# Channel mix, second product: its 98 factor loads issued from ScalarE's queue instead of SyncE's

## The chip, the cores and the metric

One core of one Trainium2 chip runs the program. The metric is the device time of one execution in microseconds (us); the kernel before was run three times.

## What is computed

Two blocks follow each other on a sequence of 1024 tokens of width 1024. The first is a recurrent mixer. The second has two layers (an RWKV-7 time mix, then a differential attention), and each layer ends in the same channel mix, which is where the change is:

```
def _sqrelu_mlp(x, w1, w2):
    return jnp.square(jax.nn.relu(x @ w1)) @ w2
...
x = _layer_norm(ALPHA * x + _sqrelu_mlp(x, mlp_w1[l], mlp_w2[l]), ln_g[l, 1], ln_b[l, 1], LN_EPS)
```

w1 is 1024 x 4096 and w2 is 4096 x 1024. Everything is float32.

## The kernel before

Every float32 product is made of three matmuls: each factor is split into a high and a low part, by a cast on ScalarE (ACT, L112) and a subtraction on VectorE (DVE, L113), and high x high, high x low and low x high are summed in PSUM.

`tail` holds a layer's channel mix and is called once for each of the two layers. Of the 4096 hidden columns, 512 go through a plain product (`direct`). The other 3584 stand in NC = 7 chunks of 512, and both products of a chunk are made by a scheme with seven products of half-size blocks in place of eight, the function `pair`: p1, p5, p2, p6, p3, and late p7 and p4, each a run of matmuls at L1549 into a PSUM bank (psx, psy or psz). Some of these sums are needed twice, so ACT copies them out of PSUM (`snap`, L1556) before TensorE (PE) goes on adding to the same bank.

- **First product** (x @ w1). Its sinks (`up_sink`) apply relu and square, form the seven sums that the second product wants as right factors, split them, and store each one to DRAM as `hd[chunk, factor]` (`parts_to`, L1500, on SyncE's queue, SP). Two stores of 512 KB make one factor of 1 MB.
- **Second product** (hidden @ w2). For each chunk, `rights(c)` loads the seven right factors from `hd` into a ring of 10 and later 12 buffers of 1 MB (names `tm`, `mxl`, `hx` in the profile): seven loads a chunk, 49 a layer, 98 in all, at L1686. The left factors come from w2 (`down_raw`, L1619, SP's queue), are summed on POOL (`lefts`, L1522) and split on ACT and DVE into `wc`. Every chunk makes four pairs of seven products of six matmuls. A buffer of the ring can be loaded again when all four pairs of its chunk have read it. The two `hx` buffers lie where the first product kept sums that it stores, so they can be filled only when those stores have landed.

A scheduler sets the order of the instructions of each engine when the program is built, and each engine then runs its own list in order. A DMA's wait is on the issuing engine's list too: what stands behind it on that engine waits with it. Completions are counted on eight semaphores in turn (`DMAHW0` to `DMAHW7` below), shared by the queues; a DMA that takes one waits until the last DMA on it has landed.

Lines that the text speaks of: L1686 the loads, L1500 the stores to `hd`, L1619 the weights of the second product, L1549 its matmuls, L1556 the copies out of PSUM, L112 the casts, L1727 the first chunk's copies into the result, L1774 eight loads of the plain product's hidden columns (`hpd`), which the change does not touch.

Of the kernel before, what the change touches and what calls it, by code (L numbers as in the profile page):

```python
# [6 lines left out]
F32 = mybir.dt.float32  # L7
# [72 lines left out]
class Net:  # L80
# [1248 lines left out]
    def tail(self, fx, wa, srcd, pre, pd, w, resd, ln1, w1, w2, ln2, outd, feats, xd, hd, hpd):  # L1329
# [8 lines left out]
        nc = self.nc  # L1338
# [4 lines left out]
        with ExitStack() as ctx:  # L1343
# [335 lines left out]
            def rights(c):  # L1679

                out = [None] * 7

                def step(i):
                    r = ring[at["ring"] % len(ring)]
                    at["ring"] += 1
                    nc.sync.dma_start(out=r.bitcast(F32), in_=hd[c, i].rearrange("p k x t -> p (k x t)"))  # L1686
                    out[i] = r.rearrange("p (k x t) -> p k x t", k=2, x=2)

                return out, [lambda i=i: step(i) for i in range(7)]
# [81 lines left out]
            for f in range(4):  # L1771
                r = ring[at["ring"] % len(ring)]
# [649 lines left out]
```

## Time and profile before

| what | value |
|---|---|
| median of 3 runs | 3378.27 us |
| lowest and highest | 3369.55 and 3382.08 us |
| the profiled execution | 3369.63 us |
| its span, first to last instruction | 3367.6 us |
| PE busy | 95% of the span |
| ACT busy | 51% |
| DVE busy | 67% |

The profile is of one execution. In the rows below, PE is the matmul engine, ACT is ScalarE, DVE VectorE, POOL GpSimd, SP SyncE; an engine's name with a q is its sequencer, as in SPq for a DMA that SP issues. Times in a timeline are microseconds from the span's start. The second product of the first layer lies at about 1735 to 2010, that of the second layer at about 3005 to 3285.

### The profile page before, as it was taken

What the parts mean: (1) busy time and instruction counts of PE and PEld (TensorE: products, weight loads), DVE (VectorE), ACT (ScalarE), POOL (GpSimd) and SP (SyncE); (2) the same over time, 40 slices, a digit from 0 to 9 for tenths busy, and PEclk for the clock granted to TensorE, in tenths of its full rate; (3) what the DMA queues carried; (4) which work ended last, traced back from release to release, by engine and by line L of the source; (5) the groups of instructions that cost most, each with busy time, mean ns of one, the idle gap of its engine ahead of it and who ended that gap; (6) DMA issues with size and microseconds to landing.
All of it is one profiled execution on the core that took longest, in us unless ns stands there. A gap on an engine that the chain in (4) does not pass through costs nothing. (4 is left out here: it accounts for less than half of the span.)

```text
span 3367.6 us, 51242 instructions
## 1 busy us (share of the span) xinstructions
PE 3193.2 (95%) x19242; PEld 2697.0 (80%) x19242; DVE 2261.9 (67%) x4255; ACT 1705.3 (51%) x3212; POOL 586.6 (17%) x463
## 2 busy tenths in 40 slices
PE   7999999989998988999999999999999999999998
PEld 5787899778777887888777887888998788777886
DVE  6645567758894867777775768226667677775777
ACT  5844235656764444466663334226566566663332
POOL 1000000000012220032224650000000032224660
PEclk9999999989997888999999999999999999999999
DMA  3110313335369655246689654544447336679653
GB/s 105 44 44 26 112 61 129 104 100 170 113 175 210 155 145 195 89 148 225 231 295 349 237 217 152 181 133 110 123 121 223 115 126 238 235 271 364 246 219 113
DMA packets 432871, 559.82 MB, mean 166 GB/s; under 512 B 114272, under 2 KB 327680, under 8 KB 419056
## 3 DMA queue, kind: packets, MB, share of 16 engines
q1 hardware_dynamic: 431792, 555.73, 50.9%
q8 instruction: 152, 2.49, 0.3%
q14 instruction: 95, 0.78, 0.1%
q0 software_dynamic: 544, 0.33, 0.0%
q10 hardware_dynamic: 288, 0.49, 0.0%
HBM read 368.25 MB, written 188.22 MB: 165 GB/s over the span
## 5 line engine op out<-in xcount | busy, mean ns | idle before, releaser
L1549 PE MATMUL psx<-tm,wc 128*128 128x512 f32 x1392 | 345.8, 390 | 4.7 <-DMA tm<-hd 2.4
L1549 PEld LDWEIGHTS psx<-tm,wc 128*128 128x128 f32 x1392 | 261.1, 188 | 62.9 <-issue 3.2
L113 DVE TENSOR_TENSOR wl<-wr,wh 128x1024 fp32r<-128x1024 f32 (+1 forms) x168 | 181.1, 1084 | 164.2 <-ACT wh L112 158.2
L112 ACT CAST wh<-wr 128x1024 fp32r<-128x1024 f32 (+1 forms) x168 | 153.9, 927 | 265.5 <-PE pskq L154 62.5
L1549 PE MATMUL psx<-mxl,wc 128*128 128x512 f32 x656 | 197.9, 390 | 0.4 <-DVE acc L100 0.4
L113 DVE TENSOR_TENSOR wc<-wr,wc 128x512 fp32r<-128x512 f32 x168 | 137.8, 823 | 51.2 <-ACT wc L112 51.2
L1549 PE MATMUL psz<-tm,wc 128*128 128x512 f32 x672 | 166.2, 389 | 0.0
L112 ACT CAST wc<-wr 128x512 fp32r<-128x512 f32 x168 | 103.6, 619 | 120.3 <-PE psz L1549 58.5
L113 DVE TENSOR_TENSOR wc<-x,wc 128x512 fp32r<-128x512 f32 x112 | 112.6, 1009 | 64.8 <-ACT wc L112 64.2
L1481 POOL TENSOR_TENSOR xx<-xx 128x512 f32<-128x512 f32 x8 | 12.0, 1498 | 820.4 <-DVE rsy L109 660.7
L153 PE MATMUL psmm<-uh,wh 128*128 128x512 f32 x384 | 152.7, 398 | 2.2 <-ACT uh L112 1.7
L1549 PE MATMUL psx<-mxh,wc 128*128 128x512 f32 x448 | 149.8, 395 | 4.4 <-DVE xx L100 4.3
L155 PE MATMUL psmm<-uh,wl 128*128 128x512 f32 x384 | 150.6, 392 | 0.5 <-DVE wl L113 0.5
L154 PE MATMUL psmm<-ul,wh 128*128 128x512 f32 x384 | 150.6, 392 | 0.5 <-DVE ul L113 0.5
L1549 PEld LDWEIGHTS psz<-tm,wc 128*128 128x128 f32 x672 | 126.2, 188 | 26.5
L1549 PEld LDWEIGHTS psx<-mxl,wc 128*128 128x128 f32 x656 | 123.0, 188 | 26.7 <-DVE acc L100 1.5
L100 DVE TENSOR_TENSOR acc<-acc,psx 128x512 f32<-128x512 f32 x144 | 96.2, 679 | 69.7 <-PE psx L1549 69.6
L993 POOL MEMSET pt<- 128x8 f32 x16 | 2.1, 128 | 724.9 <-PE psg L624 589.5
L1522 POOL TENSOR_TENSOR x<-wr 128x512 f32<-128x512 f32 x56 | 75.4, 1357 | 287.2 <-DMA wr<-in_mlp_w_dram 285.3
L112 ACT CAST wc<-x 128x512 fp32r<-128x512 f32 x112 | 69.7, 624 | 105.6 <-POOL x L1522 95.3
L97 ACT ACTIVATE e<-pss,mx 128x256 f32<-128x256 f32 (+7 forms) x128 | 94.9, 745 | 46.9 <-DVE mx L2070 26.9
L1549 PEld LDWEIGHTS psx<-mxh,wc 128*128 128x128 f32 x448 | 84.1, 188 | 29.3 <-DVE xx L100 12.1
(613 smaller groups left out, 9702.5 us busy)
## 6 DMA issues: line engine op xcount, KB each, us to landing
wr<-in_mlp_w_dram SPq DMA_DIRECT2D x128, 512.0 KB, 5.5
hd<-xx SPq DMA_DIRECT2D x112, 512.0 KB, 6.5
tm<-hd SPq DMA_DIRECT2D x50, 1024.0 KB, 7.9
mxl<-hd SPq DMA_DIRECT2D x32, 1024.0 KB, 8.1
hd<-ln SPq DMA_DIRECT2D x56, 512.0 KB, 4.0
hx<-hd SPq DMA_DIRECT2D x16, 1024.0 KB, 6.9
hd<-junk SPq DMA_DIRECT2D x28, 512.0 KB, 5.5
wr<-in_w_in_dram SPq DMA_DIRECT2D x24, 512.0 KB, 3.7
```

The source lines that it names most:

```text
L97: self.nc.scalar.activation(out=out, in_=in_, func=func, **kw)
L100: self.nc.vector.tensor_tensor(out=out, in0=a, in1=b, op=op)
L112: self.nc.scalar.copy(out=hi, in_=src)
L113: self.nc.vector.tensor_tensor(out=lo, in0=src, in1=hi.bitcast(F32), op=ALU.subtract)
L153: nc.tensor.matmul(out=ps, lhsT=ah, rhs=bh, start=first and i == 0, stop=False)
L154: nc.tensor.matmul(out=ps, lhsT=ah, rhs=bl, start=False, stop=False)
L155: nc.tensor.matmul(out=ps, lhsT=al, rhs=bh, start=False, stop=last and i == n - 1)
L993: nc.gpsimd.memset(pt[:, :, 0:1], 1.0)
L1481: nc.gpsimd.tensor_tensor(out=b0, in0=b1, in1=b0, op=ALU.subtract)
L1522: nc.gpsimd.tensor_tensor(out=s[k], in0=a, in1=b, op=op)
L1549: nc.tensor.matmul(out=ps, lhsT=a, rhs=b, start=first and k == 0 and n == 0, stop=k == nk - 1 and n == 2, skip_group_check=True,)
```

## The change

The one instruction that issues a load of a right factor moves from SP's queue to ACT's. The stores of `hd`, the loads of the weights and the loads of `hpd` stay on SP's.

```
                 def step(i):
                     r = ring[at["ring"] % len(ring)]
                     at["ring"] += 1
-                    nc.sync.dma_start(out=r.bitcast(F32), in_=hd[c, i].rearrange("p k x t -> p (k x t)"))
+
+                    nc.scalar.dma_start(out=r.bitcast(F32), in_=hd[c, i].rearrange("p k x t -> p (k x t)"))
                     out[i] = r.rearrange("p (k x t) -> p k x t", k=2, x=2)
```

Lines behind the change stand one higher in the new kernel (L1686 is L1687 there). The scheduler places the loads anew. Three places of the built programs, all in the first layer; in brackets is what a row waits for.

The first is ACT's list where the first product ends (`xx`, `ln`, `keep` are sums to be stored, `x` are copies from PSUM, `wc` left factors). Before:

```order
L112 CAST wc<-x_13045 128x512 [waits PE_49,Pool_49]
L112 CAST xx_13051<-xx_13051 128x512 [waits Activation_49]
L1556 COPY x_13043<-psz 128x512 [waits PE_49]
L112 CAST wc<-wr 128x512
L112 CAST xx_13052<-keep 128x512 [waits DMAHW4_49,DVE_49]
L112 CAST xx_13051<-xx_13051 128x512 [waits DMAHW5_49,DVE_49]
```

And with the change:

```order
L112 CAST wc<-x_13045 128x512 [waits PE_49,Pool_49]
L112 CAST xx_13051<-xx_13051 128x512 [waits Activation_49]
L1687 DMA tm_13059<-hd 128x2048 [waits PE_49]
L1556 COPY x_13043<-psz 128x512 [waits PE_49]
L112 CAST xx_13052<-keep 128x512 [waits DMAHW4_49,DVE_49]
L112 CAST wc<-wr 128x512
L1687 DMA tm_13059<-hd 128x2048
L112 CAST xx_13051<-xx_13051 128x512 [waits DMAHW5_49,DVE_49]
```

The layer's first two loads now stand behind this cast of `xx` and beside this copy of psz.

The second is SP's list at the same place, before:

```order
L1500 DMA hd<-xx_13052 128x1024 [waits DMAHW0_49,DVE_49]
L1500 DMA hd<-ln_13047 128x1024 [waits DMAHW1_49,DVE_49]
L1686 DMA tm_13059<-hd 128x2048 [waits DMAHW2_49,PE_49]
L1686 DMA tm_13059<-hd 128x2048 [waits DMAHW3_49,PE_49]
L1500 DMA hd<-ln_13048 128x1024 [waits DMAHW4_49,DVE_49,Activation_49]
L1500 DMA hd<-xx_13051 128x1024 [waits DMAHW5_49,DVE_49]
```

And with the change:

```order
L1500 DMA hd<-xx_13052 128x1024 [waits DMAHW0_49,DVE_49]
L1500 DMA hd<-ln_13047 128x1024 [waits DMAHW1_49,DVE_49]
L1500 DMA hd<-ln_13048 128x1024 [waits DMAHW4_49,DVE_49,Activation_49]
L1500 DMA hd<-xx_13051 128x1024 [waits DMAHW5_49,DVE_49]
L1500 DMA hd<-xx_13052 128x1024 [waits DMAHW6_49,DVE_49]
```

Nothing takes the two loads' place on SP: the next entry is the store of `ln` that waits for DVE and ACT.

The third is ACT's list where the second chunk's factors are fetched (`acc` is the result). Before:

```order
L1727 COPY acc<-psx 128x512 [waits PE_49]
L1556 COPY x_13044<-psx 128x512 [waits DVE_49,PE_49]
L112 CAST wc<-wr 128x512 [waits DMAHW1_49]
L112 CAST wc<-wr 128x512
L1727 COPY acc<-psx 128x512 [waits PE_49]
```

And with the change:

```order
L1728 COPY acc<-psx 128x512 [waits PE_49]
L1556 COPY x_13044<-psx 128x512 [waits DVE_49,PE_49]
L1687 DMA tm_13060<-hd 128x2048 [waits DMAHW2_49]
L1687 DMA hx_16477<-hd 128x2048 [waits DMAHW5_49,DMAHW3_49]
L1687 DMA mxl<-hd 128x2048 [waits DMAHW4_49,PE_49]
L1687 DMA mxl<-hd 128x2048 [waits DMAHW5_49,PE_49]
L112 CAST wc<-wr 128x512 x2
L1728 COPY acc<-psx 128x512 [waits PE_49]
```

Four loads, with their waits for earlier DMAs, now stand ahead of two casts of left factors.

## Rows read from the trace of the kernel before

**Rows 1.** The page's head and its list of DMA issues (count, size, median to landing)

```profile
span 3367.6 us, 51242 instructions
...
wr<-in_mlp_w_dram SPq DMA_DIRECT2D x128, 512.0 KB, 5.5
...
tm<-hd SPq DMA_DIRECT2D x50, 1024.0 KB, 7.9
```

**Rows 2.** What waited for the loads at L1686: engine, group, us, times

```profile
  PE psx L1549: 13.4, 4
```

**Rows 3.** Stretches, first layer: length, busy us by engine, PE clock, DMA share, GB/s

```profile
1735.00:1740.00 5.00, 4.97 (x23) 3.78 (x22) 2.08 (x3) 2.41 (x4) 4.84 (x4) 1.00 1.01 333
...
1750.00:1760.00 10.00, 7.60 (x31) 5.47 (x30) 7.76 (x13) 7.52 (x14) 0.00 (x0) 1.00 1.02 406
...
1800.00:1810.00 10.00, 4.44 (x14) 3.27 (x13) 1.20 (x3) 1.36 (x3) 3.05 (x3) 0.83 1.02 422
1810.00:1820.00 10.00, 10.00 (x44) 7.84 (x43) 5.21 (x8) 2.35 (x4) 3.43 (x3) 1.00 0.68 258
...
1840.00:1960.00 120.00, 120.00 (x527) 98.63 (x526) 87.87 (x108) 40.63 (x70) 72.03 (x50) 1.00 0.67 243
```

**Rows 4.** PE's timeline, both layers: start, us, line, out<-in, count, idle before

```profile
1744.77 4.24 PE L1549 MATMUL psx<-tm,wc 128*128 128x512 f32 x18
...
1798.04 2.43 PE L1549 MATMUL psz<-mxl,wc 128*128 128x512 f32 x10
1806.03 4.38 PE L1549 MATMUL psx<-hx,wc 128*128 128x512 f32 x12 [5.56 <-DMA hx<-hd]
...
3076.24 5.46 PE L1549 MATMUL psx<-hx,wc 128*128 128x512 f32 x12 [5.45 <-DMA hx<-hd]
```

**Rows 5.** SP's timeline, first layer

```profile
1734.24 1.47 SPq L1686 DMA_DIRECT2D tm<-hd  x2
1742.60 0.32 SPq L1500 DMA_DIRECT2D hd<-ln  x1
...
1790.39 0.32 SPq L1686 DMA_DIRECT2D hx<-hd  x1
...
1796.03 0.38 SPq L1619 DMA_DIRECT2D wr<-in_mlp_w_dram  x1
...
1801.28 2.09 SPq L1619 DMA_DIRECT2D wr<-in_mlp_w_dram  x1
```

**Rows 6.** Issue to landing of the loads issued at 1734.2 to 1734.9

```profile
DMA to landing us min/median/max: 7.3/8.2/9.1
```

**Rows 7.** The same for the second layer's first two, issued at 3004.5 to 3005.0

```profile
DMA to landing us min/median/max: 7.6/8.5/9.5
```

**Rows 8.** The same for the 23 loads issued between 1840 and 1980

```profile
DMA to landing us min/median/max: 4.7/6.9/9.0
```

**Rows 9.** ACT's timeline: the cast and copy around the first load's new place; a DMA issue of ACT's own

```profile
1740.74 0.62 ACT L112 CAST xx<-xx 128x512 fp32r<-128x512 f32 x1
1741.26 0.58 ACT L1556 COPY x<-psz 128x512 f32<-128x512 f32 x1
...
1.19 0.46 ACTq L179 DMA_DIRECT2D cst<-in_c_cst_dram  x1
```

**Rows 10.** Waits over the span: of SP at L1686, of POOL for the weights (us, times, longest)

```profile
SPq L1686 <- PE psx L1549: 142.3, 38, 10.1
...
POOL x L1522 <- DMA wr<-in_mlp_w_dram: 285.3, 25, 22.0
```

**Rows 11.** ACT's timeline: a copy and two casts behind later loads' new places

```profile
1769.31 0.58 ACT L1556 COPY x<-psz 128x512 f32<-128x512 f32 x1
...
1788.12 1.14 ACT L112 CAST wc<-wr 128x512 fp32r<-128x512 f32 x2
```

**Rows 12.** SP's timeline: the loads that stand ahead of them in the new list

```profile
1775.68 0.51 SPq L1686 DMA_DIRECT2D tm<-hd  x1
...
1792.60 1.24 SPq L1686 DMA_DIRECT2D mxl<-hd  x2
```

More of the change, by code (lines that the diff above doesn't have):

```diff
@@ L1685, in step @@
                     at["ring"] += 1
-                    nc.sync.dma_start(out=r.bitcast(F32), in_=hd[c, i].rearrange("p k x t -> p (k x t)"))
+                    nc.scalar.dma_start(out=r.bitcast(F32), in_=hd[c, i].rearrange("p k x t -> p (k x t)"))
                     out[i] = r.rearrange("p (k x t) -> p k x t", k=2, x=2)
```

## Prediction

> **What bounds the kernel now.** I read PE's share first, then what PE waits for in the second product, then the DMA engines there, and last the queue's own list. The span is 3367.6 us [rows 1], and the profiled execution took 3369.63 us. In the steady part of the second product, 1840 to 1960, PE is busy 120.00 of 120 us, while ACT works 40.63 of 120 [rows 3]: PE sets the pace, and nothing that arrives sooner helps. All that PE ever waited for these loads is 13.4 us in 4 waits [rows 2]. Two of them matter, one in each layer: PE stands 5.56 us before 1806.03 and 5.45 us before 3076.24 until the factor `hx` has landed [rows 4]. The reader is to see why `hx` is late. It was issued at 1790.39 [rows 5] and landed just before 1806.03, over 15 us later, where the 23 loads of the steady part take 4.7 to 9.0 us [rows 8]. The DMA engines are the reason: their share is 1.01 at 1735 to 1740, 1.02 at 1750 to 1760 and still 1.02 at 1800 to 1810, and falls to 0.68 only after 1810 [rows 3]. So from about 1735 to 1806 `hx` lies behind a backlog, and its landing is set by how much work the DMA engines have done by then.
>
> **The change part by part.** Against the profiled execution; the second layer repeats the pattern, so each term counts twice.
>
> *The first two loads start later.* SP issued them at 1734.24 and within 1.47 us [rows 5]; it then had nothing to issue until the store at 1742.60, which waits for ACT and DVE. On ACT they stand behind the cast that starts at 1740.74 and takes 0.62 us [rows 9], so the first goes out at 1741.36 at the earliest, 7.1 us later. In between the DMA engines, at 333 GB/s and a share of 1.01 [rows 3], lose these two loads as work, and SP has nothing else to give them. What is lost is two services. The two land 7.3 and 9.1 us after issues 0.6 us apart [rows 6], that is 1741.5 and 1744.0, 2.45 us apart; in the second layer 7.6 and 9.5 us after issues 0.5 apart give 2.4 [rows 7]. Two times 2.45 is 4.9 us. Since the engines have no gap until after `hx`, I take the whole 4.9 us as the shift of its landing: the wait goes from 5.56 to 10.5 us, and from 5.45 to 10.4. Bounds per layer: 0 if the hole is filled some other way, 7.1 us if the whole delay is carried on; I take 4.9, since the backlog is made of services, not of delays. **Twice 4.9 is +9.8 us.**
>
> *PE's start on the chunk.* The first load's reader is the run of psx matmuls that starts at 1744.77 [rows 4]; two matmuls in, it needs the buffer. Landing at 1741.36 plus 4.7 to 7.3 us [rows 8, 6] is 1746.1 to 1748.7, a stall of about 1 to 4 us. It costs nothing more: PE then only reaches the `hx` wait later and waits less there. Its cover is the wait of 10.5 us; without it, it would be the 1 to 4 us.
>
> *Issue time on ACT.* An issue of ACT's took 0.46 us at the start of the program [rows 9]; 98 of them are 45 us of ACT. In the steady part some 23 loads in 140 us add about 8% to an ACT that is busy 34% [rows 3], and the loads stand where ACT waits anyhow. On the path I take 0. Bounds: 0, and 0.46 for each of the some 30 loads a layer behind the `hx` wait, 14 us a layer, if every one delayed a copy that PE wants; PE's 120.00 of 120 with ACT idle two thirds of it puts the value near the lower end. Ahead of the wait the copy at 1741.26 [rows 9] is held by one issue, 0.46 us, under the same cover as above.
>
> *What SP gets back.* SP waited 142.3 us for PE's psx at these loads, with weights queued behind, and POOL waited 285.3 us for weights [rows 10]. Nobody on the path waits for POOL in the steady part, where PE is full [rows 3], so this is 0. At most the 13.4 us of [rows 2] could come back.
>
> *PE's clock.* After the wait PE runs at a lower granted clock: 0.83 over 1800 to 1810 [rows 3], and the 12 matmuls took 4.38 us in the first layer and 5.46 in the second [rows 4], against 2.43 for 10 just before, or 2.9 for 12. That loss, 1.5 and 2.6 us, is there already. A longer wait might make the first like the second, 1.1 us; I take 0.
>
> The sum is +9.8 us, 3379.4 us on the profiled execution. That lies 8.6 us under the median, so on the median I forecast **3388.1 us**.
>
> **The rivals.**
>
> *ACT is held by the loads' own waits, and PE runs out of cover.* The new list puts a load ahead of the copy of psz at 1769.31 [rows 11] that SP could issue only at 1775.68 [rows 12], because an earlier DMA on its semaphore had not landed, and four loads ahead of the casts at 1788.12 [rows 11], of which SP issued the last two by 1793.84 (1792.60 plus 1.24 [rows 12]). If those landings come as before, the first hold ends at about 1776.1, with 1.9 us of ACT's own work then still ahead of the copy: 1778.0 in place of 1769.31, 8.7 us. The second ends at 1793.9, 5.8 us late for the casts. With 2.4 us at the start that is 16.9 us by 1798, against a cover of 10.5: PE is then later than `hx`, by 16.9 less the 5.56 us it waited before, 11.3 us a layer, +22.6 in all, 3400.9 us. It decides from the point where the holds pass 10.5 us a layer. For it: each wait is written in the list. Against it: the stores on SP no longer lie behind 1 MB loads, so the landings that the holds wait for should come sooner, and a hold that ACT would have idled through is free.
>
> *The two queues share the DMA engines, and weights overtake `hx`.* Behind the load of `hx` SP issued two weight loads at 1796.03 and 1801.28 [rows 5], before `hx` had landed. In one queue they come after it; with a queue of their own they may be served beside it. 512 KB each [rows 1] at 406 GB/s [rows 3] is 1.3 us, 2.6 a layer, 5.2 on top of the forecast: 3393.3 us. The Trainium skill has a rule that would do this: DMA: Bandwidth & Descriptors, section "Queues, rings and completion order", says that each DMA engine takes its queues in turn, a packet from each. No row here shows it, as the trace of before has nearly all its traffic on one queue.
>
> *The wait for `hx` goes away: faster.* If ACT's queue is served ahead of the stores, `hx`, issued at about 1790.4, lands after a steady 4.7 to 9.0 us [rows 8], at 1795.1 to 1799.4, before PE is ready at 1800.4 (1798.04 plus 2.43 [rows 4]). That gives back 5.56 and 5.45 and the clock's 1.5 and 2.6, 15.1 us, less the start's stall, which then has no cover, 2.4 a layer: -10.3, 3368.0 us. Against it: the share of 1.02 up to 1810 [rows 3] says that the engines, not the queue's order, are short, and most of the backlog is loads of this very queue.
>
> *Nothing changes.* Stores that land sooner fill the hole, and the other places are PE's: 3378.3 us. All 98 loads do move, as the lists show, so this would be cover, not a change that was not made.
>
> **How the numbers follow.** The forecast has 0.42, the holds on ACT 0.25, the shared engines 0.13, no change 0.12, the faster case 0.08. About 0.5%, 16.9 us, is what a measurement of this kernel can tell from no change. Slower by more, over 3395.2, are the holds (0.25) and the upper edges of the forecast and of the shared engines (0.07): 0.32. Faster by more, under 3361.4, needs more than the faster case gives: 0.02. That leaves 0.66. The range reaches from just under the faster case, 3367, to just over the holds, 3402; it leaves out half of what lies beyond either, under 2 in 10. The forecast's own range is 3378 to 3398, by its bounds of 0 and 7.1 us a layer and some cost of issue.
>
> **What would show it.** In the changed profile the first loads of each layer go out at about 1741 and 3012, the DMA share dips before that and is full until about 1815, and PE waits for a load some 2 us at the start and less than 10.5 us for `hx`, both together some 10.5; at 1840 to 1960 or its counterpart PE stays full. It is wrong if the wait for `hx` shrinks with nothing in its place, if PE waits for ACT's copies (psz and psx at L1549 released by x at L1556) for more than a few us, or if the steady part has gaps.

## The result, and the profile after

| what | before | after |
|---|---|---|
| median | 3380.14 us (4 runs) | 3427.45 us (4 runs) |
| lowest and highest | 3369.55 and 3382.08 us | 3419.33 and 3436.64 us |
| the profiled execution | 3369.63 us | 3436.64 us |

The changed kernel is slower: the ratio is 1.0143, with a 95% interval of 1.0119 to 1.0168. That is +47 us against a forecast of +9.8, and above the range.

Where the time went can be read from three matmuls of each layer that stand at the same place of PE's list in all kernels below: the first at L1549, the first that reads `hx`, and the last run at L1549. PE's timeline of the kernel before (start, length, operation; the two `hx` rows stand in [rows 4]):

```profile
1452.06 0.39 PE L1549 MATMUL psx<-mxh,wc 128*128 128x512 f32 x1
...
2037.51 0.84 PE L1549 MATMUL psx<-tm,wc 128*128 128x512 f32 x3
...
2721.59 0.39 PE L1549 MATMUL psx<-mxh,wc 128*128 128x512 f32 x1
...
3308.49 0.84 PE L1549 MATMUL psx<-tm,wc 128*128 128x512 f32 x3
```

And of the changed kernel:

```profile
1466.53 0.39 PE L1549 MATMUL psx<-mxh,wc 128*128 128x512 f32 x1
...
1828.98 0.40 PE L1549 MATMUL psx<-hx,wc 128*128 128x512 f32 x1
...
2073.87 0.84 PE L1549 MATMUL psx<-tm,wc 128*128 128x512 f32 x3
...
2760.42 0.63 PE L1549 MATMUL psx<-mxh,wc 128*128 128x512 f32 x1
...
3125.25 0.63 PE L1549 MATMUL psx<-hx,wc 128*128 128x512 f32 x2
...
3375.70 0.84 PE L1549 MATMUL psx<-tm,wc 128*128 128x512 f32 x3
```

I call the way from the first of them to the `hx` matmul the **start**, and from there to the last the **rest**. The start took 353.97 and 354.65 us before, and 362.45 and 364.83 after: +8.5 and +10.2. The rest took 231.48 and 232.25 before, and 244.89 and 250.45 after: +13.4 and +18.2. Together that is +50.3. The two profiled executions differ by more, 67 us, as 14.5 of it lies ahead of the first row, in code that the change leaves alone. The executions profiled below reach that row anywhere between 1450.98 and 1467.51 us, so I compare starts and rests only.

The start has some of that drift in it too. The 1057th matmul at L1549 of each layer lies ahead of every load, and in the first layer every engine's instructions up to it are the same, in the same order. Before:

```profile
1721.80 0.50 PE L1549 MATMUL psz<-mxh,wc 128*128 128x512 f32 x1 [0.40 <-ACT x L1556]
...
2992.11 0.50 PE L1549 MATMUL psz<-mxh,wc 128*128 128x512 f32 x1 [0.40 <-ACT xa L1556]
```

And after:

```profile
1738.26 0.50 PE L1549 MATMUL psz<-mxh,wc 128*128 128x512 f32 x1 [0.43 <-ACT x L1556]
...
3033.76 0.50 PE L1549 MATMUL psz<-mxh,wc 128*128 128x512 f32 x1 [0.43 <-ACT xa L1556]
```

Counted from the first matmul of the layer that is 2.0 and 2.8 us later than before. So of the start's +18.7 us, 4.8 are drift, and 13.9 come behind that matmul.

**The wait for `hx` is gone, and others have come.** The list of PE's waits of the changed kernel has no row for `hx`, where [rows 2] had 13.4 us, 11.0 of them for `hx`. It has these instead (us, times, longest):

```profile
PE psx L1549 <- DVE xx L100: 19.1, 13, 7.5
...
PE psx L1549 <- DVE acc L100: 8.3, 14, 1.5
PE psx L1549 <- ACT xb L1556: 7.2, 3, 2.5
...
PE psx L1549 <- DMA tm<-hd: 6.9, 2, 3.5
```

**In the start**, PE's timeline has a stall on the second load, which lands at 1765.46, and then a longer one:

```profile
1765.50 5.30 PE L1549 MATMUL psx<-tm,wc 128*128 128x512 f32 x15 [3.46 <-DMA tm<-hd]
...
1782.43 0.80 PE L1549 MATMUL psx<-mxh,wc 128*128 128x512 f32 x1 [7.53 <-DVE xx L100]
```

ACT's timeline shows whose fault the 7.53 us are (ACTq is its sequencer, which issues the loads):

```profile
1771.20 0.33 ACTq L1687 DMA_DIRECT2D mxl<-hd  x1
1771.57 0.62 ACT L112 CAST xx<-xx 128x512 fp32r<-128x512 f32 x1 [5.05 <-DMA hd<-xx]
...
1779.83 0.62 ACT L112 CAST wc<-wr 128x512 fp32r<-128x512 f32 x1 [6.11 <-DMA wr<-in_mlp_w_dram]
...
1781.54 0.59 ACT L1556 COPY x<-psz 128x512 f32<-128x512 f32 x1 [0.57 <-DMA hd<-xx]
```

A load holds ACT until 1771.20, because the store that last used its semaphore has not landed. Then ACT stands until 1779.83 at a cast whose weight is late. The copy of psz, which the relu sum and so PE wait for, is behind both. The late weight was issued at 1760.86 and took 18.9 us to land; the same weight took 6.6 us before. Other weights of the start, issued later, took up to 18.8 us in the kernel before as well.

**In the rest**, which was full before [rows 3], PE has gaps: those over 0.15 us sum to 11.0 us in the first layer and 12.4 in the second. The other 8 to 9 us of the loss are matmuls that took longer; the mean granted clock of the second layer's rest is 0.97, in place of 0.99 before. A stretch of 120 us behind the `hx` matmul, and one of 10 us around a gap of the second layer (length, busy us of PE, PEld, DVE, ACT and POOL, PE clock, DMA share, GB/s):

```profile
1862.00:1982.00 120.00, 113.27 (x480) 90.19 (x479) 85.53 (x105) 36.83 (x64) 73.64 (x51) 0.99 0.61 221
...
3150.00:3160.00 10.00, 7.65 (x26) 5.74 (x25) 4.40 (x3) 2.83 (x5) 6.16 (x4) 0.83 0.58 215
```

In the long stretch ACT has less to do than before and the DMA engines are less busy, so neither is short of time as a whole. One gap, by the timelines of SP, ACT and PE, shows the cause:

```profile
1847.16 0.37 SPq L1619 DMA_DIRECT2D wr<-in_mlp_w_dram  x1
...
1847.59 0.33 ACTq L1687 DMA_DIRECT2D tm<-hd  x1
...
1850.22 0.33 ACTq L1687 DMA_DIRECT2D mxl<-hd  x1
...
1857.46 0.62 ACT L112 CAST wc<-wr 128x512 fp32r<-128x512 f32 x1 [5.34 <-DMA wr<-in_mlp_w_dram]
1857.99 0.58 ACT L1556 COPY x<-psx 128x512 f32<-128x512 f32 x1
...
1858.62 1.67 PE L1549 MATMUL psx<-tm,wc 128*128 128x512 f32 x6 [2.01 <-ACT x L1556]
```

What these three DMAs took from issue to landing, the weight first:

```profile
DMA to landing us min/median/max: 10.3/10.3/10.3
...
DMA to landing us min/median/max: 6.5/6.5/6.5
...
DMA to landing us min/median/max: 7.1/7.1/7.1
```

The weight of 512 KB was issued first and landed last, at 1857.4; the loads of 1 MB issued behind it landed at 1854.1 and 1857.3. In the kernel before the same weight landed after 4.2 us. ACT stands at its cast, and the copy that PE wants is the next on ACT's list. The other gaps of the rest that I followed are of this kind, some by way of the sums that POOL makes of the weight: ACT's cast of a sum is late, and with it DVE's addition into `acc` that frees a PSUM bank.

The page's list of DMA queues says what sets loads and weights apart (packets, MB, share; q1 is SP's, q10 is ACT's). Before and after:

```profile
q10 hardware_dynamic: 288, 0.49, 0.0%
```

```profile
q1 hardware_dynamic: 417680, 452.96, 42.2%
q10 hardware_dynamic: 14400, 103.26, 7.8%
```

ACT's queue now moves 103.26 MB in 14400 packets, 7.2 KB each on average. SP's moves 452.96 MB in 417680, 1.1 KB each. A load reads 8 KB in one piece for each partition, a weight 256 columns of float32, 1 KB.

What the two queues moved in part of the gap above, 1851 to 1855 us, while the weight and the loads were under way:

```profile
q10 hardware_dynamic: 177, 1.32, 84.0%
q1 hardware_dynamic: 254, 0.25, 17.8%
```

The weight's queue got more packets through than the loads', and less than a fifth of their bytes. In the 2 us before 1849 it had moved 520 packets, with hardly anything beside it.

### The profile page after: what moved, and what is told of

The parts are those of the page before. It is cut to its first block, busy times and chain, and to the rows that moved or that the text cites. A ratio compares the mean times of both kernels' runs of the same rounds, so it can differ in the third digit from the quotient of the medians.

```text
span 3434.9 us, 51203 instructions
## 1 busy us (share of the span) xinstructions
PE 3228.3 (94%) x19242; PEld 2718.8 (79%) x19242; DVE 2259.9 (66%) x4255; ACT 1702.6 (50%) x3212; POOL 584.1 (17%) x463
## 3 DMA queue, kind: packets, MB, share of 16 engines
q1 hardware_dynamic: 417680, 452.96, 42.2%
q10 hardware_dynamic: 14400, 103.26, 7.8%
## 4 chain that ended last, share of the span: by engine, by line
PE 39%; DMA 11%; DVE 8%; issue 3%; ACT 3%; POOL 3%; SPq 0%; POOLq 0%; DVEq 0%; ACTq 0%
PE psx L1549 10%; DMA wr<-in_mlp_w_dram 8%; PE psz L1549 4%; PE psy L1549 2%; PE pskq L153 2%; PE pskq L155 2%; PE pskq L154 2%; PE psd L153 2%; PE psd L154 2%; PE psd L155 2%; DVE wc L113 1%; PE po L2111 1%; PE pz L1208 1%; POOL x L1522 1%; PE pm L1160 1%
## 5 line engine op out<-in xcount | busy, mean ns | idle before, releaser
L1549 PE MATMUL psx<-tm,wc 128*128 128x512 f32 x1392 | 354.4, 398 | 22.1 <-ACT xb L1556 7.2
L1549 PEld LDWEIGHTS psx<-tm,wc 128*128 128x128 f32 x1392 | 265.4, 192 | 85.4 <-ACT xb L1556 8.5
L1549 PE MATMUL psx<-mxl,wc 128*128 128x512 f32 x656 | 201.0, 394 | 3.8 <-DVE acc L100 2.6
L1549 PE MATMUL psx<-mxh,wc 128*128 128x512 f32 x448 | 153.6, 404 | 19.5 <-DVE xx L100 19.1
L1549 PE MATMUL psz<-tm,wc 128*128 128x512 f32 x672 | 167.2, 391 | 2.5 <-DVE acc L100 2.5
L1481 POOL TENSOR_TENSOR xx<-xx 128x512 f32<-128x512 f32 x8 | 12.4, 1552 | 818.9 <-PE psd L155 663.9
L1549 PEld LDWEIGHTS psz<-tm,wc 128*128 128x128 f32 x672 | 126.5, 188 | 29.6 <-DVE acc L100 2.9
L1549 PEld LDWEIGHTS psx<-mxl,wc 128*128 128x128 f32 x656 | 124.3, 190 | 32.2 <-DVE acc L100 3.1
L1549 PEld LDWEIGHTS psx<-mxh,wc 128*128 128x128 f32 x448 | 86.7, 194 | 46.4 <-DVE xx L100 28.2
```

The costliest lines, as they stand in the source:

```text
L1549: nc.tensor.matmul(out=ps, lhsT=a, rhs=b, start=first and k == 0 and n == 0, stop=k == nk - 1 and n == 2, skip_group_check=True,)
```

## The experiments

**Theory 1**: two queues share the DMA engines piece by piece, so loads in pieces of 8 KB starve a weight in pieces of 1 KB, and ACT stands at that weight's cast. **Theory 2**: ACT is held by the waits of the loads in its own list. All medians, with the change in the start and in the rest of both layers together against the kernel before, taken from the same rows as above. Each ratio is to runs of the kernel before that were made beside it (medians 3380.14 to 3384.42 us). Start and rest are from one execution of each kernel; "drift" is the part of the start's change that lies ahead of the 1057th matmul.

| kernel | median us | ratio to before, interval | start | of it drift | rest |
|---|---|---|---|---|---|
| the changed kernel | 3427.45 | 1.0143 (1.0119 to 1.0168) | +18.7 | +4.8 | +31.6 |
| 1 KB pieces, loads on ACT | 3418.23 | 1.0096 (1.0067 to 1.0125) | +37.2 | +5.2 | -1.0 |
| 1 KB pieces, loads on SP | 3404.06 | 1.0064 (1.0043 to 1.0085) | +21.4 | +7.5 | +4.0 |
| chunks 2 to 6 on ACT | 3407.65 | 1.0072 (1.0046 to 1.0098) | +9.1 | +2.4 | +19.2 |
| chunks 0 and 1 on ACT | 3393.73 | 1.0029 (1.0016 to 1.0043) | +18.3 | +6.2 | +3.6 |
| loads and weights on ACT | 3395.78 | 1.0037 (1.0018 to 1.0057) | +19.1 | +2.3 | -5.0 |
| 2 KB weights, loads on ACT | 3400.74 | 1.0059 (1.0035 to 1.0083) | +19.6 | +1.8 | +5.0 |
| 2 KB weights, loads on SP | 3394.66 | 1.0039 (1.0027 to 1.0051) | +3.4 | -0.7 | +12.6 |
| first two loads on ACT | 3387.39 | 1.0025 (1.0007 to 1.0043) | +9.3 | +1.6 | +0.3 |
| first `hx` load on ACT | 3387.92 | 1.0010 (0.9997 to 1.0023) | -4.0 | +4.8 | +12.8 |
| two `hx` loads on ACT | 3392.07 | 1.0019 (1.0005 to 1.0033) | -3.1 | +2.8 | +16.0 |
| chunks 1 to 6 and weights on ACT | 3392.76 | 1.0022 (1.0006 to 1.0038) | +13.2 | +1.7 | -4.0 |
| rows of the layer norm held back | 3379.13 | 0.9989 (0.9974 to 1.0004) | -1.2 | +2.0 | -1.5 |

In the two kernels with 1 KB pieces the stores ahead of that matmul differ as well, so there the drift can be in part their own.

**The length of the pieces.** A gap in `hd`'s layout makes loads, and stores to `hd`, move in pieces of 1 KB; nothing else changes, and the order of all instructions stays:

```
-dram("hd", [7, 7, P, 2, 2, H2])
+dram("hd", [7, 7, P, 2, 4, 272])
...
-parts_to(x, x[:, 1] if f is None else f, hd[c, n, :, i])
+parts_to(x, x[:, 1] if f is None else f, hd[c, n, :, i, :, 0:256], 4)
...
-nc.scalar.dma_start(out=r.bitcast(F32), in_=hd[c, i].rearrange("p k x t -> p (k x t)"))
+nc.scalar.dma_start(out=r.bitcast(F32).rearrange("p (j t) -> p j t", j=8), in_=hd[c, i].rearrange("p k j t -> p (k j) t")[:, :, 0:256])
```

> The changed kernel with `hd` laid out in DRAM with a gap after every 1 KB, so that each load of a factor (and each store to `hd`) moves in runs of 1 KB, as the weights do, in place of 8 KB (4 KB for the stores). The order of every engine's instructions is that of the changed kernel. Theory 1 (the two queues share the DMA engines run by run, so a 1 MB load in 8 KB runs starves a 512 KB weight in 1 KB runs; ACT then stands at the cast of that weight with a copy behind it that PE wants): the weights that took 10.3, 14.5, 14.5 and 18.9 us to land come back to 5 to 9 us, PE's gaps in the later, steady part of each layer's second product (13 us a layer) mostly go, and the time falls to 3395 to 3410 us. Theory 2 (ACT is held by the loads' own waits, or simply by 98 more issues): weights may land as they like, the gaps stay, 3420 to 3440 us. Either way the run of the same layout on SyncE's queue is to be taken off.

The control, with `nc.sync` in that line:

> The kernel before (loads on SyncE's queue) with the same gapped layout, 1 KB runs; the order of all instructions is that of the kernel before. It prices the layout itself. Both theories: one queue serves its DMAs in order, so the length of a run should matter only where the DMA engines are full (1735 to 1810 us and its like in the second layer). If short runs move at the same rate: 3375 to 3385 us; if they are slower, the landing of `hx` is later, up to some 10 us a layer: 3400 us.

The rest is back to what it was before, -1.0 in place of +31.6, although all loads are still on ACT, at the same places of its list. Stores can't be the reason, as the last store to `hd` of the layer is issued ahead of the rest. A stretch of 120 us of the rest:

```profile
1850.00:1970.00 120.00, 118.83 (x517) 96.51 (x518) 91.95 (x111) 40.84 (x72) 74.13 (x52) 1.00 0.78 245
```

The packets of ACT's queue, now 1 KB each:

```profile
q10 hardware_dynamic: 102208, 103.26, 9.4%
```

The landing of the 20 weights of the rest of the first layer, in the kernel before:

```profile
DMA to landing us min/median/max: 3.3/5.0/10.0
```

in the changed kernel:

```profile
DMA to landing us min/median/max: 3.3/5.2/14.5
```

and with pieces of 1 KB, loads on ACT:

```profile
DMA to landing us min/median/max: 3.4/6.5/8.7
```

The median got worse, and the DMA engines are busier with the same bytes (share 0.78 against 0.67 in [rows 3]), but none is late. In the second layer the slowest takes 8.6 us, against 15.1 in the changed kernel. Only the start keeps the time from the 3395 to 3410 us that was expected: it costs 37.2 on ACT and 21.4 on SP. The control's 3404.06 us is nearest to the second case of its expectation. With the layout's price taken off, the loads on ACT cost 3418.23 - 3404.06 = 14 us in place of 47. For the rest this is what theory 1 asks for, and what theory 2 excludes. In the start it is not so: without the drift, the loads on ACT cost 18.1 us more than on SP with pieces of 1 KB (32.0 less 13.9), and 13.9 with pieces of 8 KB. The length of the pieces is not shown to be what the start loses by.

**Which loads.** Both parts of the change by themselves:

```
-nc.scalar.dma_start(out=r.bitcast(F32), ...)
+(nc.scalar if c > 1 else nc.sync).dma_start(out=r.bitcast(F32), ...)
```

> Only the loads of chunks 2 to 6 (35 of each layer's 49) on ScalarE's queue, those of chunks 0 and 1 on SyncE's. If the gaps of the steady part are made by loads of the steady part (theory 1 and theory 2 agree on that), the start of each layer is as before (a wait for `hx` of some 5.5 us) and the steady part has gaps of some 13 us a layer: 3380 + 26 = about 3406 us (3395 to 3415). If instead the steady part suffers from the late start only (a chain that never recovers), it is full again: 3375 to 3385 us.

and with `nc.sync if c > 1 else nc.scalar`:

> Only the loads of chunks 0 and 1 (14 of each layer's 49) on ScalarE's queue, the rest on SyncE's. By the changed kernel's trace the start then has a stall of some 3.5 us and the one of 5 to 7.5 us before the relu sums, in place of the wait for `hx` of 5.5 us, with some time more at the lower clock: 3380 + 2 x (11.8 - 5.5 + 3) = about 3399 us (3388 to 3405), and a full steady part. The forecast on record (the first two loads lost as services, all of the change in the start) would also put all of the loss here, with a wait for `hx` of some 10 us.

Chunks 2 to 6 alone lose 19.2 us in the rest, as expected, though not all of 31.6; chunks 0 and 1 alone keep it nearly full (+3.6) and lose 18.3 in the start, 6.2 of it drift. That profiled execution is the slowest of ten (3406.77 us, the next 3396.61), and the median moves by 9.3 only, so the size of this start is uncertain. The medians of the two parts move by 23.2 and 9.3, together 32.5 of the 47: the parts are not simply additive. The start of chunks 2 to 6, expected as before, lost 9.1. It holds theory 2's mechanism in a pure form. ACT's row behind the load, and PE's:

```profile
1785.09 0.33 ACTq L1687 DMA_DIRECT2D tm<-hd  x1
1785.47 0.60 ACT L97 ACTIVATE junk<-psx 128x512 f32<-128x512 f32 x1 [8.09 <-DMA hd<-ln]
...
1786.12 0.79 PE L1549 MATMUL psx<-tm,wc 128*128 128x512 f32 x1 [5.98 <-ACT junk L97]
```

One load, waiting for a store on its semaphore, keeps ACT idle 8.09 us, and PE 5.98 (6.33 in the second layer).

**Loads and weights in one queue.** The weights follow the loads to ACT:

```
 down_raw:
-nc.sync.dma_start(
+nc.scalar.dma_start(
     out=x, in_=w2[c * FC : c * FC + FC, o : o + 256].rearrange("(k p) f -> p k f", p=P)
```

> The loads and the weights of the second product (L1619) both on ScalarE's queue, 8 KB and 1 KB runs as in the changed kernel; the stores stay on SyncE's. Theory 1 (queues share the DMA engines by run, weights starve beside loads of the other queue): loads and weights are now in one queue and are served in order, so no weight of the steady part takes over 10.5 us to land and the steady part's loss falls from 35 us (14.85 and 20.09) to under 10; the start costs some 11 us as in the changed kernel: 3390 to 3405 us. Theory 2 (ScalarE is held by the waits of DMAs in its list): it now holds the weights' waits too, which were over 100 us of SyncE's time in a layer: slower than the changed kernel, over 3435 us.

The time is in theory 1's range. ACT's list now holds the 98 loads and the second product's weights, with all their waits, and the rest is full:

```profile
1825.00:1945.00 120.00, 120.00 (x526) 98.31 (x525) 90.07 (x113) 41.92 (x73) 82.05 (x55) 1.00 0.66 245
```

The slowest of its 20 weights in the first layer takes 9.2 us (10.3 in the second):

```profile
DMA to landing us min/median/max: 3.3/5.4/9.2
```

So in the rest neither the issues nor the holds on ACT cost anything. In the start they do: PE waits 4.99 and 4.76 us for an activation that stands on ACT's list behind the DMA of a weight, which in turn waits for a load on its semaphore to land. The rest is even 5.0 shorter than before, as there is no wait for `hx` and so no slow matmuls behind it (4.38 and 5.46 us against 2.9 for 12 at full clock, [rows 4], 4 us for both layers).

**Longer pieces for the weights.** A weight's tile takes 2 row blocks of 512 columns:

```
-x = wa.tile([P, 4, 256], F32, tag="wr", ...)
+x = wa.tile([P, 2, 512], F32, tag="wr", ...)
...
-nc.sync.dma_start(out=x, in_=w2[c * FC : c * FC + FC, o : o + 256].rearrange("(k p) f -> p k f", p=P))
+nc.sync.dma_start(out=x, in_=w2[o : o + 256, H2 * g : H2 * g + H2].rearrange("(k p) f -> p k f", p=P))
```

> The changed kernel with the weights of the second product loaded in runs of 2 KB in place of 1 KB (a tile of two row blocks of 512 columns in place of four of 256; the casts, subtractions and sums read it as 2 x 256). Theory 1: a weight gets twice the share beside an 8 KB load, so what it takes over the usual 5 us is about halved (14.5 to about 10 us), and of the steady part's 35 us half or more goes: 3400 to 3412 us. Theory 2: the holds on ScalarE are the same, 3420 to 3440 us.

> The kernel before with weights in runs of 2 KB, the control of the run above. In one queue the length of the weights' runs should not matter in the steady part (PE is full there). Where the DMA engines are full, some six weights of 512 KB lie ahead of `hx`; if longer runs save them a third of their time, `hx` is 2 to 3 us sooner in each layer: 3370 to 3382 us.

The loads on ACT now cost 6 us more than on SP (3400.74 less 3394.66), in place of 47, and the rest +5.0 in place of +31.6: theory 1's direction, and more than the half expected. The control missed. The waits for `hx` fell to 3.17 and 3.95 us, but `hx` took 15.4 and 16.5 us to land after its issue, no less than the 15.5 and 15.3 before: it is PE that came later. And each sum now needs both tiles of a pair, and PE waits for casts of weights just behind `hx`, up to 3.47 us. So the size of this result counts for less than its sign.

**The step that the forecast charged.**

```
-nc.scalar.dma_start(out=r.bitcast(F32), ...)
+(nc.scalar if c == 0 and i < 2 else nc.sync).dma_start(out=r.bitcast(F32), ...)
```

> Only the first two loads of each layer on ScalarE's queue, all others on SyncE's. This is the one step that the forecast on record charged: two services of 2.45 us lost by the DMA engines in each layer, the wait for `hx` 5.5 to some 10.5 us, +9.8 us: 3385 to 3395 us. If the hole is filled by other transfers, the wait for `hx` stays at 5.5 us and the time at 3378 to 3384 us.

The start costs 4.7 and 4.6 us, 9.3 in all and 7.7 without the drift, and the median moves by 6.3. A stretch in which the DMA engines lack the two loads:

```profile
1750.00:1760.00 10.00, 7.16 (x29) 4.92 (x28) 8.04 (x13) 7.14 (x14) 2.24 (x2) 1.00 0.65 216
```

PE's timeline at its two waits in the first layer:

```profile
1761.39 5.29 PE L1549 MATMUL psx<-tm,wc 128*128 128x512 f32 x15 [3.73 <-DMA tm<-hd]
...
1821.74 1.62 PE L1549 MATMUL psx<-hx,wc 128*128 128x512 f32 x3 [6.42 <-DMA hx<-hd]
```

The two waits together are 10.15 us (10.22 in the second layer), against the 10.5 that the forecast gave for both. Before, PE already stood 1.2 us at a load there, 6.8 us with the wait for `hx` (6.7 in the second layer).

**Only `hx` on ACT.** Can the wait for `hx` be had back without the loss?

```
-nc.scalar.dma_start(out=r.bitcast(F32), ...)
+(nc.scalar if c == 1 and i == 3 else nc.sync).dma_start(out=r.bitcast(F32), ...)
```

> Only one load of each layer, that of the first `hx` factor (chunk 1, factor 3), on ScalarE's queue; the 48 others, weights and stores stay on SyncE's. The lists of TensorE, VectorE and GpSimd are those of the kernel before. Theory 1 (a transfer in the other queue does not stand behind the first queue's backlog, but shares the DMA engines with it, with 8 KB runs against 1 and 4 KB): `hx`, issued at about 1790, lands within 5 to 9 us, before TensorE wants it at 1800.4, and the waits of 5.56 and 5.45 us go, with some of the time at the lower clock behind them: 11 to 15 us less than the kernel before, 3366 to 3371 us. If the DMA engines serve in the order of issue across queues, the waits stay: 3378 to 3384 us.

> The first two `hx` loads of each layer (chunk 1, factors 3 and 4) on ScalarE's queue. As the run above; the second `hx` was issued some 8 us behind the first and nobody waited for it in the kernel before. If in the run above the second `hx` becomes the one that is waited for, this one is faster by that wait; if not, the two are the same within 3 us. A second load beside the weights issued at 1796 and 1801 can starve them: a wait of TensorE's of 1 to 3 us behind a cast of a left factor would show it.

`hx` landed 9.3 us after its issue, and the wait for it went; the expected time did not come, and the interval does not tell the kernel from the one before. The timelines of PE and of ACT, and a stretch between:

```profile
1819.17 2.97 PE L1549 MATMUL psx<-hx,wc 128*128 128x512 f32 x12
...
1834.26 1.22 PE L1549 MATMUL psx<-tm,wc 128*128 128x512 f32 x2 [6.65 <-ACT wc L112]
...
1833.59 1.14 ACT L112 CAST wc<-wr 128x512 fp32r<-128x512 f32 x2 [10.78 <-DMA wr<-in_mlp_w_dram]
```

```profile
1820.00:1830.00 10.00, 7.61 (x34) 5.88 (x32) 2.81 (x5) 1.17 (x2) 4.37 (x4) 1.00 1.01 415
```

The DMA engines are still full at 1820 to 1830, and the weight behind `hx` pays: PE waits 6.65 us for it (6.41 in the second layer) in place of 5.5 for `hx`. Counted from the first matmul of the layer, the last weight of the backlog lands at 366.6 us before, and here at 369.8, or 367.5 without the 2.4 us of drift. So the backlog ended at much the same point, and whoever was last in it waited. The second `hx` load on ACT made it no better.

**Chunk 0 on SP, the rest of the loads and the weights on ACT** (`c > 0`):

> The loads of chunk 0 (7 of each layer's 49) on SyncE's queue as before, the other 42 and the weights of the second product on ScalarE's. Against the run with all loads and weights on ScalarE's queue this takes away the stall at the start (some 4 us a layer) and leaves ScalarE's hold of 5 us a layer behind a load that waits for an earlier landing. If that hold is the rest of the loss: 8 us less than that run, 3383 to 3390 us, with a full steady part. If the start's loads made the hold too, it goes with them: 3366 to 3375 us.

The start is 5.9 us shorter than with all loads and weights on ACT (5.3 without the drift) and the rest full. That is in the direction of the first expectation, but the two medians lie only 3 us apart with intervals that overlap: inconclusive for the time.

**Less backlog.** Two loads of 512 KB that nobody needs yet wait for a late value:

```
 if c == 3:
+    for k in range(2):
+        nc.gpsimd.tensor_copy(out=lnr[k][:, 0:1], in_=accs[0][:, 0, 0:1])
     rows(lnr[0], ln2[0])
     rows(lnr[1], ln2[1])
```

> All loads on SyncE's queue as in the kernel before; what moves is the two loads of the layer norm's rows (L1392, 512 KB each), which stood just ahead of `hx` on SyncE's list. A copy of one column on GpSimd, from the result into the rows' buffer, holds them back until chunk 2 is summed, by when the DMA engines have room. If the wait for `hx` is the backlog of the DMA engines and nothing else, 1 MB less of it is worth the 2.45 us between two landings of such a size: the wait of some 5.5 us falls to about 3, in both layers, and the time by 5 to 7 us against the kernel before. If `hx` waits for its own stores or for its place in the queue only, the wait stays at 5.5 us and the time is the same.

PE's waits for `hx` in this kernel, first and second layer:

```profile
1816.13 0.64 PE L1549 MATMUL psx<-hx,wc 128*128 128x512 f32 x1 [3.68 <-DMA hx<-hd]
...
3087.25 0.47 PE L1549 MATMUL psx<-hx,wc 128*128 128x512 f32 x1 [2.02 <-DMA hx<-hd]
```

They fall by 1.9 and 3.4 us, but not all of that is `hx` coming sooner. From the issue of the layer's first load to the landing of `hx` it is 70.0 us in both layers, in place of 71.7 and 71.6: 1.6 us sooner, not the expected 2.45. The remainder of the shorter waits is PE coming to `hx` later. The median falls by 3.6 us, which the interval does not tell from no change. It has the lowest median of the versions here, and it leaves the loads on SP.

## Why the prediction was wrong

*The first two loads start later, +9.8.* Right in its mechanism, where it stands alone, and somewhat large: the run of these two loads has 7.7 us in the start without the drift and 6.3 in the median, with both waits together 10.2, near the 10.5 of the forecast. In the changed kernel it is not the whole of the start.

*The wait for `hx` grows.* Wrong in the changed kernel: it vanished, but not as the rival of the faster case said. Counted from the first matmul of the layer, `hx` landed at 359.4 and 361.5 us, 5.6 and 7.0 later than before (3.6 and 4.2 without the drift): issued later, it took 9.7 and 9.4 us to land in place of 15.5 and 15.3. So the landing did shift by about the 4.9 us that the forecast had. But PE came to `hx` at 362.6 and 365.0, in place of 348.4 and 349.2, after the stall on the second load and the 7.53 us behind ACT. It had run out of cover, as the rival of ACT's holds said, and the -10.3 us of the faster case did not come.

*ACT is held by the loads' own waits.* This rival named the right place. The whole start costs +18.7, 13.9 without the drift, against the +22.6 that it gave. By the run of the first two loads some 8 of the 13.9 may be theirs; how the others divide between holds and late weights is open. That a hold alone can stop PE is shown by the run of chunks 2 to 6 (5.98 us) and that of loads and weights in one queue (4.99).

*Issue time on ACT, 0.* Right in the steady part: 120.00 us of PE in 120 with loads and weights all on ACT.

*PE's clock, 0.* Short: 8 to 9 us of the rest's loss are matmuls that took longer, behind PE's gaps. Over 3150 to 3160, where PE is busy 7.65 of 10 us, the granted clock is 0.83, a mean of its full and its lower level. The forecast looked for this behind the wait for `hx` alone.

*What SP gets back, 0, with PE full in the steady part.* This is the step that failed, together with the rival of the shared engines. The forecast let the steady part stay full on the ground that it was full before, and priced the sharing in one direction alone: weights that overtake `hx`, as equals, 5.2 us. The traces show the other direction: loads overtake weights, because a load's pieces are eight times as long, and ACT's list stands until the weight is there. That is +31.6 us, the larger part of the loss, and -1.0 once the pieces are of one length. [rows 1] and [rows 8] showed two kinds of transfers that took 5.5 and 6.9 us (medians) in one queue; nothing in the price of either said what happens when each has a queue of its own, and I should have put a bound of several late weights a layer there.

That the engines take the queues in turn, a packet from each, is what the Trainium skill says in DMA: Bandwidth & Descriptors, section "Queues, rings and completion order", and what the forecast cited. The runs lean that way: with loads in pieces of 1 KB beside weights of 1 KB no weight of the first layer's rest took over 8.7 us, with pieces of 8 KB one took 14.5. Strict turns they do not show: of the profile's packets, one for each contiguous piece, the weight's queue moved 254 and the loads' 177 from 1851 to 1855. By the page a packet is a group of descriptors; whether the profile counts the same thing is in no record here. So the sharing went by the piece more than by the byte, and the forecast had priced it by the byte.

## What to carry to other kernels

Before a transfer gets a queue of its own, compare the length of its contiguous pieces with those of what stays behind. Here pieces of 8 KB won over pieces of 1 KB, and as ACT's list stood at the shorter ones, a queue that was nearly idle before still cost 31.6 us. The loads on a compute engine's queue were harmless in the rest, once the weights shared their queue, and held ACT for 5 to 8 us where one of them stood until an earlier DMA on its semaphore had landed. And the wait at the end of a full backlog was not removed by priority: it went from `hx` to a weight. 1 MB less in the backlog brought `hx` 1.6 us sooner.

## What was not expected of the hardware

A DMA of 512 KB issued 0.4 us ahead of one of 1 MB on the other queue landed 3.3 us behind it (10.3 us against 6.5), although the share of the DMA engines fell from 1.03 at 1850 to 1854 us to 0.52 at 1854 to 1858, while it was still on its way. That half of the engines' time was free and the weight still late is not explained by theory 1, nor by any run here. And the same bytes in pieces of 1 KB in place of 8 raised the share of the DMA engines in the rest from 0.67 to 0.78, with the median of a load's landing in 1860 to 2000 us rising from 6.9 to 8.9 us.
